# Gate biases as a 3-row product instead of an addition on VectorE, and the turn of the inverses pinned behind a weight split

## The chip, the core and the metric

The kernel runs on one core of a Trainium2 chip. A core has a matrix engine (TensorE, PE in the rows; its weight loads are PEld), a vector engine (VectorE, DVE), a scalar engine for functions (ScalarE, ACT), GpSimd (POOL) and SyncE (SP), which here only issues DMAs. Each engine works through its own instructions in a fixed order and waits at an instruction until its operands are there; all that stands behind it waits too. The metric is the device time of one execution in microseconds (us); the median of three runs is compared.

## What is computed

The reference is a stack of two blocks on 256 tokens of 2048 channels, in fp32. The first has two attention layers. The second is the one that the change touches:

```python
def second_block(x, ...):
    h = rms_norm(x, norm_w[i])
    proj = h @ w_in[i]
    (g_qkv, g_z, g_b, g_a, r_feat, r_z, s_u, s_z, gate_logits) = _split_cols(proj, SPLIT_SIZES)
    o_a = gdn_branch(...)        # gated delta rule in chunks of 64, with triangular solves
    o_b = rwkv7_branch(...)      # a second recurrence with the same kind of solve
    o_c = s5_branch(...)         # a diagonal state space
    branch_proj = einsum('blnc,ncd->blnd', [o_a, o_b, o_c], w_branch[i])
    gates = sigmoid(gate_logits.reshape(bsz, seq, N_BRANCH, D_MODEL) + gate_b[i])
    merged = sum(gates * branch_proj, axis=2)
    x = x + merged @ w_out[i]
    return rms_norm(x, final_norm_w)
```

There are 3 x 2048 gate columns, each with a bias in `gate_b`.

## The kernel before

Nearly all of the work is projections: activations times a weight matrix that is read from HBM. To keep fp32 accuracy, each number is split into a high and a low part, and a projection makes three products (high by high, high by low, low by high) of 512 columns each, or the like of it. The generator `weights` (line 185) loads a projection's weights in parts: a raw part (`raw`, 512 KB, six buffers), a cast to the high part on ACT (`wh`, L167), and a subtraction for the low part on DVE (`wl`, L124), three buffers each. A group of 512 gate columns has 8 such parts of 12 products each. The raw loads go through SP's queue, in a fixed order, among all other loads and stores that SP issues.

`projT` (line 262) is the projection that the gates use: 256 tokens in two halves, accumulated in a PSUM tile `pj` of which there are two, so that one group is evacuated while the next accumulates. `gates` (line 1555) runs it for 12 groups: nine in a row (0, 1, 2, 4, 5, 6, 8, 9, 10), then 11, 7 and 3, each right after a `z_gate` projection and ahead of the branch products that use the result (`in_w_branch`). The activations in SBUF are not yet divided by the norm, so that a group's evacuation multiplies by the token's factor `r` and adds the bias, which a DMA has spread over 128 partitions (`gb`, out of the tile ring `ev` with four buffers), takes tanh of half of it, and stores the result to a DRAM tile `gates`.

Beside the projections, chains of small steps run as generators (`Flow`): the recurrences. Their steps are put into the program by a clock that counts TensorE's columns: `yield LAT["inv"]` means that the chain goes on after 32 us of products. `inverse64` (line 1106) inverts 64 x 64 triangles, six times in the program. It writes them to DRAM and reads their 16 x 16 diagonal blocks (`uim`, `LB`), inverts these in some 20 small DVE operations on `b` (the last is a reduction, L1142), sends the result through DRAM again (`dim`, then two loads of `e`, both on ACT's queue), turns `e` by a transposition on DVE (L1149), and then needs four products with the turned blocks. The first of these, `ps<-e,d`, comes after the `inv` delay.

The order of instructions on each engine is made by a scheduler from priorities; `high_priority(offset=...)` moves weight loads and evacuations ahead, `issue_after(i)` puts what is in its block behind the instruction `i` on the same engine.

Of the kernel before, what the change touches and what calls it, by code (L numbers as in the profile page):

```python
# [8 lines left out]
F32 = mybir.dt.float32  # L9
F32R = mybir.dt.float32r  # L10
AF = mybir.ActivationFunctionType
ALU = mybir.AluOpType
# [10 lines left out]

LAT = dict(small=12.0, bc=8.5, fd=10.0, fb=1.2, fh=0.8, z=0.3, sm=8.85, pt=1.42, st=6.0, ix=0.55, top=9.0, s5=11.0, inv=32.0, pr=1.3,
           prz=1.6, feat=15.0, prod=2.2, c1=1.25, c3=1.3, gn=11.0, sc=6.5, conv=22.5, ln=4.1, rw=2.3, rb=9.0, gp=1.0,
           kt=1.0, gu=3.25, gc=1.3, gR=1.5, go=1.0, gg=7.2)

# [32 lines left out]
class Ker:  # L62
# [122 lines left out]
    def weights(self, w, blocks, nk=KT, pool=None, KC=KC):  # L185
        runs, off = [], 0
        for c0, n in [r for b in blocks for r in (b if isinstance(b, list) else [b])]:
            if runs and runs[-1][0] + runs[-1][1] == c0:
                runs[-1][1] += n
            else:  # L190
                runs.append([c0, n, off])
            off += n
        for kc in range(0, nk, KC):
          self.ahead(kc)
          with self.tc.high_priority(offset=self.HP), self.linked():
            raw = self.t(self.pw, [128, KC, off], "raw", bufs=6)
            for c0, n, o in runs:
                d = self.nc.sync.dma_start(
                    raw[:, :, o:o + n],
                    w[kc * 128:(kc + KC) * 128, c0:c0 + n].rearrange("(k p) c -> p k c", p=128))  # L200
            h, l = (self.t(pool or self.pw, [128, KC, off], tag, F32R, bufs=8 if pool else 3) for tag in ("wh", "wl"))
            i = self.split(h, l, raw)
          if self.order:
              self.order = [d.ins] + i
          yield kc, h, l
# [53 lines left out]
        self.after()  # L259


    def projT(self, w, c0, n, x, evac, nk=KT):
        xh, xl = x
        pt = self.t(self.pp, [128, 2, 512], "pj")
        for kc, h, l in self.weights(w, [(c0, n)], nk):
            for k in range(self.KC):
                kk = kc + k
                for t in range(2):
                    ts = slice(t * 128, t * 128 + 128)
                    st, sp = kk == 0, kk == nk - 1  # L270
                    self.mm(pt[:, t, 0:n], xh[:, kk, ts], h[:, k, 0:n], st, False)
                    self.mm(pt[:, t, 0:n], xh[:, kk, ts], l[:, k, 0:n], False, False)
                    self.mm(pt[:, t, 0:n], xl[:, kk, ts], h[:, k, 0:n], False, sp)
                    self.tick()
        if self.must is not None:
            self.drain(self.must)
        with self.tc.high_priority(offset=self.HPE):
            evac(pt)
        self.after()
# [635 lines left out]
class Block2:  # L915
# [188 lines left out]
    def inverse64(self, pl, usrc, C, turn, n=8):  # L1104
# [41 lines left out]
        for d in range(2):  # L1146
            dma(D2[64 * d:64 * d + 64, 0], at(di, d * n * 4160, [[64, 64], [4160, n], [1, 64]]))
        D2 = [D2[:, 0], D2[:, 1]]
        nc.vector.transpose(D2[1].rearrange("p n s -> p (n s)"), D2[0].rearrange("p n s -> p (n s)"))  # L1149
        d4, c4 = K.t(pl, [128, 2, n, 64], "d4"), K.t(pl, [128, 2, n, 64], "c4")  # L1150
        Uo, NT, Y, Z = d4[:, 0], d4[:, 1], c4[:, 0], c4[:, 1]
        for d in range(2):
            rows = slice(64 * d, 64 * d + 64)
            K.tt(Uo[rows], usrc(d, rows), C["off"][rows].unsqueeze(1).to_broadcast([64, n, 64]), ALU.mult)

        def prod(l, r):
            p = K.ps()
# [3 lines left out]
                    rows = slice(64 * d, 64 * d + 64)  # L1161
                    K.mm(pv[rows, i], l[rows, i], r[rows, i])
            return pv
        yield LAT["inv"]
        nc.scalar.copy(NT, prod(Uo, D2[1]))
        yield LAT["pr"]
        nc.scalar.copy(Y, prod(NT, D2[0]))
# [384 lines left out]
            K.act(self.o[0][:, hs, c * 128:c * 128 + 128], pv4(p), AF.Copy, scale=prm["gnw"])  # L1552


    def gates(self, groups, dst):
        K, nc = self.K, self.nc
        bias = self.a["gate_b_2"][0].rearrange("n c -> (n c)")
        for gi in groups:
            def evac(pt, gi=gi):
                e = K.t(self.pe, [128, 2, 512], "ev")  # L1560
                gb = K.t(self.pe, [128, 2, 512], "ev")[:, 0]
                nc.sync.dma_start(gb, bias[gi * 512:gi * 512 + 512].partition_broadcast(128))
                for t in range(2):
                    K.stt(e[:, t], pt[:, t], self.r[:, t:t + 1], gb, ALU.mult, ALU.add)
                K.act(e, e, AF.Tanh, scale=0.5)
                nc.sync.dma_start(dst[gi], e)
            K.projT(self.w, 10448 + gi * 512, 512, self.x, evac)

    def z_gate(self, pl, i, c0, factor, need=None):
        K = self.K  # L1570
# [99 lines left out]
def second_block(K, x1, yt, w_out1, T, prm):  # L1670
# [39 lines left out]
    with ExitStack() as e2:  # L1710
        gd = K.t(K.pd, [12, 128, 2, 512], "gates")
        with ExitStack() as e3:
            B = Block2(K, xt, r2, rbc, e3)
            pcn = K.pool("b2c", 1, e3)
            C = block2_consts(K, pcn, prm)
            pr = K.pool("rec", 1, e3)
            B.images(pr)
            e4 = ExitStack()
            ps5 = K.pool("s5", 1, e4)
            f, wl, al, baz, rn, feats = B.rwkv_feats(pcn, prm, C)  # L1720
            B.out(1)
            gq = K.t(K.pd, [24, 128, S], "gqkv")
            feats(0)
            nf, nr = [1], [0]

            def chains():
                for q in range(4):
                    while nf[0] <= q:
                        yield 1.0
                    yield from B.rwkv(pr, q, f, wl, al, rn, prm, C)  # L1730
                    nr[0] += 1
                B.out(0)
                sc = yield from B.gdn_scalars(pcn, baz, C)
                while B.nq < 6:
                    yield 1.0
                for hf in range(2):
                    yield from B.gdn(pr, hf, gq, sc, prm, C)
                    yield
            main = K.flow(chains(), (0,))
            B.s5_u()  # L1740
            side = K.flow(B.s5(ps5, T, prm), (1,))
            for q in range(1, 4):
                feats(q)
                nf[0] = q + 1
            for g in range(6):
                B.gdn_qkv(gq, (g,))
            B.gates((0, 1, 2, 4, 5, 6, 8, 9, 10), gd)
            K.drain(side)
            B.s5_glu(prm)
            for i, n in enumerate(("d_o0", "d_o1", "d_o2")):  # L1750
                if n in a:
                    nc.sync.dma_start(a[n].rearrange("b p s -> p b s"), B.o[i])
            e4.close()
            pz = K.pool("zs", 1, e3)
            acc = K.t(K.pd, [4, 128, 2, 512], "acc")
            o2 = B.z_gate(pz, 2, 9424, 0.125)
            B.gates((11,), gd)
            B.branch(2, o2, gd, acc)
            while nr[0] < 4:
                main.step()  # L1760
            o2 = B.z_gate(pz, 1, 7376, 0.5)
            B.gates((7,), gd)
            B.branch(1, o2, gd, acc)
            o2 = B.z_gate(pz, 0, 3072, 0.5, lambda g: K.drain(main, g + 1))
            K.drain(main)
            B.gates((3,), gd)
            m = K.xtiles("x")
            B.branch(0, o2, gd, acc, m)
# [120 lines left out]
```

## Time and profile before

| | |
|---|---|
| median of three runs | 2176.87 us (2176.57 to 2179.06) |
| profiled execution | 2182.66 us |
| its span, first to last instruction | 2180.6 us |
| busy share of PE, DVE, ACT, POOL | 97%, 77%, 48%, 2% |
| granted clock of TensorE, mean | 0.992 |
| DMA | 440 MB at 202 GB/s |

The durations below come from the one profiled execution. A row of a timeline says when an instruction began, how long it took, its engine (a small q is the engine's queue, which issues a DMA), its line in the kernel, what it writes and reads (buffer numbers left out), and, in brackets, how long the engine had idled before and what ended that.

### The profile page before, as it was taken

How to read it: one execution, taken by the hardware profiler on the slowest of the kernel's cores; microseconds unless marked ns; L12 is line 12 of the kernel's file. 1: busy time of each engine (PE TensorE's matmuls, PEld its weight loads, DVE VectorE, ACT ScalarE, POOL GpSimd, SP SyncE). 2: the span in 40 equal slices, each digit the busy share in tenths (PEclk: the TensorE clock that was granted, in tenths of full speed). 3: DMA queues.
4: the chain of work that ended last, by engine and by line, in shares of the span. 5: the costliest groups of instructions: out<-in, count | busy, mean ns of one | idle time of the engine just before them, and what ended most of it. 6: DMA issues, size and time to landing. Idle time of an engine off the chain costs nothing. (4 is left out here: it accounts for less than half of the span.)

```text
span 2180.6 us, 32801 instructions
## 1 busy us (share of the span) xinstructions
PE 2120.5 (97%) x12275; PEld 1792.8 (82%) x12275; DVE 1670.1 (77%) x2919; ACT 1043.7 (48%) x1498; POOL 53.5 (2%) x113
## 2 busy tenths in 40 slices
PE   9999999999999999999999999999999989989998
PEld 8888898888898888888888778777678868868886
DVE  6788866668999777565789999989888848765665
ACT  5445554544454455555544434334346635525443
POOL 2001000000000000000000000000000000000000
PEclk9999999999999999999999999999999999999999
DMA  7666656766667756876676676665856657775874
GB/s 251 196 181 176 170 155 184 245 207 213 203 180 206 221 158 183 279 221 197 191 223 199 196 207 206 202 206 177 230 164 191 195 190 208 237 215 156 274 231 148
DMA packets 356143, 440.09 MB, mean 202 GB/s; under 512 B 50380, under 2 KB 262528, under 8 KB 355664
## 3 DMA queue, kind: packets, MB, share of 16 engines
q1 hardware_dynamic: 328240, 430.81, 65.4%
q10 hardware_dynamic: 26512, 4.68, 1.2%
q0 software_dynamic: 1232, 2.51, 0.4%
q8 instruction: 96, 1.57, 0.3%
q14 instruction: 63, 0.52, 0.1%
HBM read 396.35 MB, written 41.57 MB: 201 GB/s over the span
## 5 line engine op out<-in xcount | busy, mean ns | idle before, releaser
L167 ACT CAST wh<-raw 128x1024 fp32r<-128x1024 f32 (+4 forms) x668 | 683.8, 1026 | 857.1 <-PE pj L141 713.6
L124 DVE TENSOR_TENSOR wl<-raw,wh 128x1024 fp32r<-128x1024 f32 (+4 forms) x668 | 794.3, 1191 | 341.1 <-ACT wh L167 332.8
L141 PE MATMUL pj<-x,wh 128*128 128x512 f32 (+3 forms) x3008 | 1019.2, 387 | 0.7 <-ACT wh L167 0.7
L141 PE MATMUL pj<-x,wl 128*128 128x256 f32 (+2 forms) x2864 | 807.4, 282 | 2.3 <-DVE wl L124 2.3
L141 PEld LDWEIGHTS pj<-x,wh 128*128 128x128 f32 (+2 forms) x3008 | 554.2, 187 | 125.7 <-issue 9.2
L141 PEld LDWEIGHTS pj<-x,wl 128*128 128x128 f32 (+2 forms) x2864 | 539.9, 189 | 9.0 <-issue 4.0
L141 PE MATMUL pj<-wh,x 128*128 128x512 f32 (+2 forms) x1472 | 451.2, 382 | 0.0
L141 PEld LDWEIGHTS pj<-wh,x 128*128 128x128 f32 x1472 | 271.8, 189 | 46.6 <-issue 2.9
L141 PE MATMUL pj<-wl,x 128*128 128x512 f32 (+2 forms) x736 | 279.5, 380 | 1.2 <-DVE wl L124 1.2
L141 PEld LDWEIGHTS pj<-wl,x 128*128 128x128 f32 x736 | 138.6, 188 | 25.7 <-DVE wl L124 2.1
L141 PE MATMUL pj<-wh,y 128*128 128x512 f32 x512 | 158.4, 390 | 0.0
L141 PEld LDWEIGHTS pj<-wh,y 128*128 128x128 f32 x512 | 95.9, 188 | 19.8
L141 PE MATMUL pj<-wl,y 128*128 128x512 f32 x256 | 99.9, 390 | 0.0
L141 PE MATMUL pj<-wl,E 128*128 128x512 f32 x192 | 77.2, 402 | 2.6 <-DVE wl L124 2.6
L141 PE MATMUL pj<-wh,E 128*128 128x512 f32 x192 | 77.4, 403 | 2.1 <-ACT wh L167 2.1
L141 PE MATMUL pj<-wh,G 128*128 128x512 f32 x192 | 77.1, 402 | 0.0
L124 DVE TENSOR_TENSOR raw<-y 128x256 f32<-128x256 f32 (+7 forms) x256 | 64.0, 289 | 3.0
L141 PEld LDWEIGHTS pj<-wl,y 128*128 128x128 f32 x256 | 48.1, 188 | 9.9
L124 DVE TENSOR_TENSOR y<-raw 128x128 f32<-128x128 f32 (+7 forms) x256 | 46.2, 223 | 2.5
L141 PEld LDWEIGHTS pj<-wl,E 128*128 128x128 f32 x192 | 36.7, 191 | 12.0 <-DVE wl L124 4.8
L141 PEld LDWEIGHTS pj<-wh,E 128*128 128x128 f32 x192 | 36.6, 191 | 10.4 <-ACT wh L167 2.5
L124 DVE TENSOR_TENSOR s5w<-ps,s5tb 128x512 f32<-128x512 f32 x64 | 42.6, 683 | 3.2 <-PE ps L141 3.1
(457 smaller groups left out, 1998.3 us busy)
## 6 DMA issues: line engine op xcount, KB each, us to landing
raw<-in_w_in_dram SPq DMA_DIRECT2D x460, 512.0 KB, 3.7
raw<-in_w_out_dram SPq DMA_DIRECT2D x96, 512.0 KB, 4.7
raw<-in_w_branch_dram SPq DMA_DIRECT2D x48, 512.0 KB, 4.6
raw<-in_w_in_dram SPq DMA_DIRECT2D x24, 344.0 KB, 3.2
s5t<-y SPq DMA_DIRECT2D x16, 512.0 KB, 5.7
s5tb<-s5t SPq DMA_DIRECT2D x32, 256.0 KB, 3.6
raw<-in_w_in_dram SPq DMA_DIRECT2D x16, 384.0 KB, 3.6
gates<-ev SPq DMA_DIRECT2D x12, 512.0 KB, 3.6
```

The source lines that it names most:

```text
L124: return (eng or self.nc.vector).tensor_tensor(out=out, in0=a, in1=b, op=op)
L141: i = self.nc.tensor.matmul(out, l, r, start=st, stop=sp, **k)
L167: i = self.nc.scalar.copy(h, src)
```

## The change

It has two parts. The gate biases enter as the first product of a group's accumulation: three rows (high, high and low part of the bias against the high, low and high part of the tokens' divisors 1/r), so that ACT can make the tanh straight from PSUM with a factor r/2 per token. A new function `gate_bias` prepares both once: the biases' parts are written to a DRAM tile `gbr`, and each group loads its three rows of 512 (6 KB) from there into an `ev` tile. In the inverses, the transposition is moved behind the `inv` delay, which grows from 32 to 34 us, and is pinned behind the latest weight split on DVE (`lastw`); a further delay `turn` of 2.5 us lies between it and the first product.

```diff
@@ -23,7 +23,7 @@
 
 
 
-LAT = dict(small=12.0, bc=8.5, fd=10.0, fb=1.2, fh=0.8, z=0.3, sm=8.85, pt=1.42, st=6.0, ix=0.55, top=9.0, s5=11.0, inv=32.0, pr=1.3,
+LAT = dict(small=12.0, turn=2.5, bc=8.5, fd=10.0, fb=1.2, fh=0.8, z=0.3, sm=8.85, pt=1.42, st=6.0, ix=0.55, top=9.0, s5=11.0, inv=34.0, pr=1.3,
            prz=1.6, feat=15.0, prod=2.2, c1=1.25, c3=1.3, gn=11.0, sc=6.5, conv=22.5, ln=4.1, rw=2.3, rb=9.0, gp=1.0,
            kt=1.0, gu=3.25, gc=1.3, gR=1.5, go=1.0, gg=7.2)
 
@@ -200,6 +200,7 @@
                     w[kc * 128:(kc + KC) * 128, c0:c0 + n].rearrange("(k p) c -> p k c", p=128))
             h, l = (self.t(pool or self.pw, [128, KC, off], tag, F32R, bufs=8 if pool else 3) for tag in ("wh", "wl"))
             i = self.split(h, l, raw)
+            self.lastw = i[1]
           if self.order:
               self.order = [d.ins] + i
           yield kc, h, l
@@ -259,15 +260,18 @@
         self.after()
 
 
-    def projT(self, w, c0, n, x, evac, nk=KT):
+    def projT(self, w, c0, n, x, evac, nk=KT, bias=None):
         xh, xl = x
         pt = self.t(self.pp, [128, 2, 512], "pj")
+        if bias is not None:
+            for t in range(2):
+                self.mm(pt[:, t, 0:n], bias[0][t], bias[1], True, False)
         for kc, h, l in self.weights(w, [(c0, n)], nk):
             for k in range(self.KC):
                 kk = kc + k
                 for t in range(2):
                     ts = slice(t * 128, t * 128 + 128)
-                    st, sp = kk == 0, kk == nk - 1
+                    st, sp = kk == 0 and bias is None, kk == nk - 1
                     self.mm(pt[:, t, 0:n], xh[:, kk, ts], h[:, k, 0:n], st, False)
                     self.mm(pt[:, t, 0:n], xh[:, kk, ts], l[:, k, 0:n], False, False)
                     self.mm(pt[:, t, 0:n], xl[:, kk, ts], h[:, k, 0:n], False, sp)
@@ -1146,12 +1150,15 @@
         for d in range(2):
             dma(D2[64 * d:64 * d + 64, 0], at(di, d * n * 4160, [[64, 64], [4160, n], [1, 64]]))
         D2 = [D2[:, 0], D2[:, 1]]
-        nc.vector.transpose(D2[1].rearrange("p n s -> p (n s)"), D2[0].rearrange("p n s -> p (n s)"))
         d4, c4 = K.t(pl, [128, 2, n, 64], "d4"), K.t(pl, [128, 2, n, 64], "c4")
         Uo, NT, Y, Z = d4[:, 0], d4[:, 1], c4[:, 0], c4[:, 1]
         for d in range(2):
             rows = slice(64 * d, 64 * d + 64)
             K.tt(Uo[rows], usrc(d, rows), C["off"][rows].unsqueeze(1).to_broadcast([64, n, 64]), ALU.mult)
+        yield LAT["inv"]
+
+        with K.tc.issue_after(K.lastw):
+            nc.vector.transpose(D2[1].rearrange("p n s -> p (n s)"), D2[0].rearrange("p n s -> p (n s)"))
 
         def prod(l, r):
             p = K.ps()
@@ -1161,7 +1168,7 @@
                     rows = slice(64 * d, 64 * d + 64)
                     K.mm(pv[rows, i], l[rows, i], r[rows, i])
             return pv
-        yield LAT["inv"]
+        yield LAT["turn"]
         nc.scalar.copy(NT, prod(Uo, D2[1]))
         yield LAT["pr"]
         nc.scalar.copy(Y, prod(NT, D2[0]))
@@ -1552,19 +1559,44 @@
             K.act(self.o[0][:, hs, c * 128:c * 128 + 128], pv4(p), AF.Copy, scale=prm["gnw"])
 
 
+    def gate_bias(self):
+
+
+        K, nc = self.K, self.nc
+        self.gbr = K.t(K.pd, [12, 3, 512], "gbr")
+        b = K.t(self.pe, [128, 2, 512], "ev")[0:12, 0]
+        nc.sync.dma_start(b, self.a["gate_b_2"][0].rearrange("n (q c) -> (n q) c", c=512))
+        bp = K.t(self.pe, [128, 2, 512], "ev", F32R)[0:12]
+        K.split(bp[:, 0], bp[:, 1], b)
+        for i, part in enumerate((0, 0, 1)):
+            nc.sync.dma_start(self.gbr[:, i], bp[:, part].bitcast(F32))
+        inv, h, c = K.t(K.pc, [128, 2], "rinv"), K.t(K.pc, [128, 2, 2], "rinvp", F32R), K.t(K.pc, [128, 2, 3], "rinvc")
+        nc.vector.reciprocal(inv, self.r)
+        K.split(h[:, 0], h[:, 1], inv)
+        for i, part in enumerate((0, 1, 0)):
+            nc.vector.tensor_copy(c[:, :, i], h[:, part].bitcast(F32))
+        p = K.ps()
+        self.rdiv = []
+        for t in range(2):
+            K.tr(p[0:3, 128 * t:128 * t + 128], c[:, t])
+            self.rdiv.append(K.t(K.pc, [128, 128], "dg", F32R, bufs=2)[0:3])
+            nc.scalar.copy(self.rdiv[t], p[0:3, 128 * t:128 * t + 128])
+        self.rhalf = K.t(K.pc, [128, 2], "rhalf")
+        K.ts(self.rhalf, self.r, 0.5, None, ALU.mult)
+
     def gates(self, groups, dst):
         K, nc = self.K, self.nc
-        bias = self.a["gate_b_2"][0].rearrange("n c -> (n c)")
         for gi in groups:
+            with K.tc.high_priority(offset=K.HP):
+                gb = K.t(self.pe, [128, 2, 512], "ev")[0:3, 0]
+                nc.sync.dma_start(gb, self.gbr[gi])
+
             def evac(pt, gi=gi):
                 e = K.t(self.pe, [128, 2, 512], "ev")
-                gb = K.t(self.pe, [128, 2, 512], "ev")[:, 0]
-                nc.sync.dma_start(gb, bias[gi * 512:gi * 512 + 512].partition_broadcast(128))
                 for t in range(2):
-                    K.stt(e[:, t], pt[:, t], self.r[:, t:t + 1], gb, ALU.mult, ALU.add)
-                K.act(e, e, AF.Tanh, scale=0.5)
+                    K.act(e[:, t], pt[:, t], AF.Tanh, scale=self.rhalf[:, t:t + 1])
                 nc.sync.dma_start(dst[gi], e)
-            K.projT(self.w, 10448 + gi * 512, 512, self.x, evac)
+            K.projT(self.w, 10448 + gi * 512, 512, self.x, evac, bias=(self.rdiv, gb.bitcast(F32R)))
 
     def z_gate(self, pl, i, c0, factor, need=None):
         K = self.K
@@ -1721,6 +1753,7 @@
             B.out(1)
             gq = K.t(K.pd, [24, 128, S], "gqkv")
             feats(0)
+            B.gate_bias()
             nf, nr = [1], [0]
 
             def chains():
```

What moved is seen in three places of the program. The first is SP's queue at the gate group 11. `raw` of `in_w_in` are the group's weight loads, `raw` of `in_w_branch` those of the branch products that follow, `ev<-in_gate_b` and `ev<-gbr` the load of the group's bias. Before:

```order
L198 DMA raw_16676<-in_w_in_dram 128x2x512
L198 DMA raw_16730<-in_w_in_dram 128x2x512
L198 DMA raw_16766<-in_w_in_dram 128x2x512
L198 DMA raw_16803<-in_w_in_dram 128x2x512
L198 DMA raw_16849<-in_w_branch_dram 128x2x512
L1562 DMA ev_16842<-in_gate_b_dram 128x512
L198 DMA raw_16885<-in_w_branch_dram 128x2x512
L198 DMA raw_16909<-in_w_branch_dram 128x2x512
```

After:

```order
L198 DMA raw_16751<-in_w_in_dram 128x2x512
L198 DMA raw_16769<-in_w_in_dram 128x2x512
L198 DMA raw_16792<-in_w_branch_dram 128x2x512
L1592 DMA ev_16638<-gbr_10051 3x512
L198 DMA raw_16810<-in_w_branch_dram 128x2x512
L1415 DMA b_2918_17380<-gqkv_9854 128x4x256
L198 DMA raw_16829<-in_w_branch_dram 128x2x512
```

The bias load, smaller now and from another place, stands behind the first weight load of the next projection in both. Such is its place in groups 11, 7 and 3; in the eight others after the first, it comes behind the group's eighth weight load, and in the first one behind its fourth.

The second place is TensorE at the beginning of the same group: `pj` is the accumulator, `x` the activations, `wh` and `wl` the split weights; `ev` is the loaded bias and `dg` the turned divisors. Before:

```order
L141 MATMUL pj_16505<-x_8492,wl_16575 128x256
L141 MATMUL pj_16505<-x_8492,wh_16574 128x512
L141 MATMUL pj_16505<-x_8492,wl_16575 128x256
L141 MATMUL pj_16603<-wh_16606,x_8492 128x512
L141 MATMUL pj_16603<-wl_16607,x_8492 128x512
L141 MATMUL pj_16603<-wh_16606,x_8492 128x512 x2
L141 MATMUL pj_16603<-wl_16607,x_8492 128x512
```

After:

```order
L141 MATMUL pj_16501<-x_8492,wh_16609 128x512
L141 MATMUL pj_16501<-x_8492,wl_16610 128x256
L141 MATMUL pj_16640<-ev_16638,dg_10071 128x512
L141 MATMUL pj_16640<-ev_16638,dg_10074 128x512
L141 MATMUL pj_16640<-wh_16645,x_8492 128x512
L141 MATMUL pj_16640<-wl_16646,x_8492 128x512
L141 MATMUL pj_16640<-wh_16645,x_8492 128x512 x2
```

Two products that read the loaded bias are now ahead of the group's first product with weights.

The third place is DVE in the fifth inverse, from the last reduction on `b` to the transposition of `e`. `wl` are weight splits of the projections beside it, and the row at L127 with `r` is a gate group's evacuation. Before:

```order
L1142 TENSOR_REDUCE b_2741_16364<-b_2741_16364 64x8x8
L124 TENSOR_TENSOR wl_16852<-raw_16849,wh_16851 128x1024
L124 TENSOR_TENSOR wl_16888<-raw_16885,wh_16887 128x1024
L127 SCALAR_TENSOR_TENSOR ev_16841<-pj_16603,r_1500_9225,ev_16842 128x512 x2
L124 TENSOR_TENSOR wl_16912<-raw_16909,wh_16911 128x1024
L124 TENSOR_TENSOR wl_16951<-raw_16948,wh_16950 128x1024
L1149 STREAM_TRANSPOSE e_2743_16390<-e_2743_16390 128x512
L124 TENSOR_TENSOR wl_16974<-raw_16971,wh_16973 128x1024
L124 TENSOR_TENSOR c_2745_16395<-ps_2796_16745,e_2743_16390 128x512
```

After:

```order
L1146 TENSOR_REDUCE b_2770_16518<-b_2770_16518 64x8x8
L124 TENSOR_TENSOR wl_16700<-raw_16697,wh_16699 128x1024
L124 TENSOR_TENSOR wl_16718<-raw_16715,wh_16717 128x1024
L124 TENSOR_TENSOR wl_16736<-raw_16733,wh_16735 128x1024
L124 TENSOR_TENSOR wl_16754<-raw_16751,wh_16753 128x1024
L124 TENSOR_TENSOR wl_16772<-raw_16769,wh_16771 128x1024
L124 TENSOR_TENSOR wl_16795<-raw_16792,wh_16794 128x1024
L124 TENSOR_TENSOR wl_16813<-raw_16810,wh_16812 128x1024
L1161 STREAM_TRANSPOSE e_2772_16544<-e_2772_16544 128x512
L124 TENSOR_TENSOR wl_16832<-raw_16829,wh_16831 128x1024
```

The transposition has gone from behind four weight splits to behind seven, and the evacuation's rows are gone.

## Rows read from the trace of the kernel before

**Rows 1.** The page: the span, and part 1, busy time of the engines.

```profile
span 2180.6 us, 32801 instructions
...
PE 2120.5 (97%) x12275; PEld 1792.8 (82%) x12275; DVE 1670.1 (77%) x2919; ACT 1043.7 (48%) x1498; POOL 53.5 (2%) x113
```

**Rows 2.** Chain of waits, TensorE's own: us in total, times, longest.

```profile
PE ps L141 <- DVE e L1149: 20.6, 5, 6.9
PE pj L141 <- DVE wl L124: 6.2, 9, 1.1
```

**Rows 3.** The line of the transposition: what its engine idled for (us, times).

```profile
  DMA e<-dim: 21.7, 6
```

**Rows 4.** Timeline around the fifth inverse, all engines.

```profile
1745.22 0.68 DVE L1142 TENSOR_REDUCE b<-b 64x64 f32<-64x512 f32 x1
...
1760.41 0.71 DVE L1149 STREAM_TRANSPOSE e<-e 128x512 f32<-128x512 f32 x1 [6.92 <-DMA e<-dim]
...
1761.17 1.12 PE L141 MATMUL ps<-e,d 64*64 64x64 f32 x16 [6.86 <-DVE e L1149]
```

**Rows 5.** Stretches after TensorE's waits: length, PE busy, PEclk, DMA share, GB/s.

```profile
1430.60:1436.00 5.40, 5.40 (x54) 0.57 0.80 271
...
1938.00:1944.50 6.50, 6.47 (x59) 0.55 0.66 174
1278.60:1283.00 4.40, 4.35 (x84) 1.00 0.78 231
```

**Rows 6.** Chain of waits of ACT, and of SP's queue.

```profile
ACT wh L167 <- PE pj L141: 713.6, 450, 7.0
...
SPq L198 <- DVE wl L124: 1046.4, 457, 9.8
```

**Rows 7.** Timeline of PE and SP, begin of groups 11 and 3.

```profile
1726.46 0.39 PE L141 MATMUL pj<-wh,x 128*128 128x512 f32 x1
1726.69 0.40 PE L141 MATMUL pj<-wl,x 128*128 128x512 f32 x1
...
1729.30 0.46 SPq L1562 DMA_DIRECT2D ev<-in_gate_b_dram  x1
...
2014.88 0.40 PE L141 MATMUL pj<-wh,x 128*128 128x512 f32 x1
...
2017.72 0.46 SPq L1562 DMA_DIRECT2D ev<-in_gate_b_dram  x1
```

**Rows 8.** Timeline of SP and DVE, begins of two of the other groups.

```profile
1393.50 0.47 SPq L1562 DMA_DIRECT2D ev<-in_gate_b_dram  x1
...
1397.39 0.74 DVE L127 SCALAR_TENSOR_TENSOR ev<-pj,r,ev 128x512 f32<-128x512 f32 x1
...
1618.93 0.46 SPq L1562 DMA_DIRECT2D ev<-in_gate_b_dram  x1
...
1619.71 1.41 DVE L127 SCALAR_TENSOR_TENSOR ev<-pj,r,ev 128x512 f32<-128x512 f32 x2 [0.29 <-PE pj L141]
```

**Rows 9.** DMA issues: KB each, median us from issue to landing.

```profile
raw<-in_w_in_dram SPq DMA_DIRECT2D x460, 512.0 KB, 3.7
...
ev<-in_gate_b_dram SPq DMA_DIRECT2D x12, 256.0 KB, 4.2
...
y<-in_norm_dram SPq DMA_DIRECT2D x1, 8.0 KB, 1.6
```

**Rows 10.** Stretch of group 3: length, busy of PE, PEld, DVE, ACT, POOL.

```profile
2014.00:2037.00 23.00, 23.00 (x104) 19.08 (x104) 15.62 (x15) 11.08 (x12) 0.00 (x0) 1.00 0.64 199
```

**Rows 11.** Groups by line: busy, mean ns of one, idle before, releaser.

```profile
L167 ACT CAST wh<-raw 128x1024 fp32r<-128x1024 f32 (+4 forms) x668 | 683.8, 1026 | 857.1 <-PE pj L141 713.6
L124 DVE TENSOR_TENSOR wl<-raw,wh 128x1024 fp32r<-128x1024 f32 (+4 forms) x668 | 794.3, 1191 | 341.1 <-ACT wh L167 332.8
...
L136 ACT ACTIVATE ev<-ev 128x1024 f32<-128x1024 f32 x18 | 19.0, 1058 | 6.4 <-DVE ev L124 3.8 <-DVE ev L127 2.6
...
L127 DVE SCALAR_TENSOR_TENSOR ev<-pj,r,ev 128x512 f32<-128x512 f32 x24 | 17.1, 743 | 1.8 <-PE pj L141 1.6
```

## The prediction

> **What bounds the kernel now.** I began with the busy rows: TensorE is busy in 97% of the span [rows 1], so the bound is the row of matrix products, and a change is worth what it adds to that row or takes out of its gaps. Of about 60 us of gaps, the list of TensorE's waits names one large cause: 20.6 us in five waits for the turn of the inverses (DVE's transposition of `e`), while all waits of the projections (`pj`) for weight splits come to 6.2 us [rows 2]. The transposition waited 21.7 us for its DMAs [rows 3]: DVE stands at it, and TensorE's next instruction stands behind DVE. In the fifth inverse the last reduction begins at 1745.22 (ends 1745.9), the turn at 1760.41 after 6.92 us of idling, and TensorE has stood for 6.86 us [rows 4]. From the end of the reduction to the turn that is 14.5 us.
>
> A stall costs more than its length. After the waits in the third to sixth inverse (3.3 to 6.9 us) the granted clock fell to its lower level of 1.2 GHz for a while: a mean of 0.57 over 5.4 us in the first of these four, of 0.55 over 6.5 us in the last; after the wait in the second inverse (1.6 us) it stayed at 1.00 [rows 5]. Stretch times one minus the clock gives 5.4 x 0.43 = 2.3 and 6.5 x 0.45 = 2.9 us, and 9.5 us for all four, 2.4 each. So the inverses cost 20.6 + 9.5 = 30.1 us.
>
> The last view is of what paces the loads. ACT's casts wait for TensorE (713.6 us), and the queue that issues the weights waits for DVE's splits (1046.4 us) [rows 6]. Thus TensorE's own progress sets when a load is issued: six raw buffers and three split buffers are a ring.
>
> **The change, part by part.**
>
> *Bias products.* Each of the 12 gate groups gets two more products of 512 columns. Such a product starts 0.23 us after the one before (1726.46 to 1726.69 [rows 7]): 24 x 0.23 = 5.5 us. No product of 3 rows stands in the trace; bounds are 0 and this 128-row spacing, and I take the spacing, since the width is the same. The Trainium skill ("TensorE: Matmul & The Clock Gate", Why this matters for your kernels) says that a single product with 32 rows takes as long as one with 128; by that it is 5.5 us too, and no run here shows it.
>
> *The bias load: the deciding term.* Before, the bias was needed at a group's end, some 20 us after its load. Now it is the first operand of the group, since its product opens the accumulation. But the order of SP's queue hardly moves: in 8 groups the new load stands behind the group's eighth and last weight load, in three (11, 7, 3) behind the next projection's first as well; only in the first group is it earlier (behind the fourth). Those weight loads can't be issued early. The eighth needs the second's raw buffer, hence the second split, hence a split buffer that TensorE frees only with the previous group's seventh part; the ninth needs the eighth part of the previous group to be finished.
>
> The old load stood at the same places, so its rows tell when. In the three late groups TensorE began the first at 1726.46 and the last at 2014.88, and their loads were issued at 1729.30 and 2017.72: 2.84 us later in both [rows 7]. In the eight others I compare its issue with the previous group's evacuation, which starts when that group ends: 1393.50 against 1397.39 in the first, 1618.93 against 1619.71 in the last; the mean of the eight is -1.0 us [rows 8], about -0.8 against TensorE's own start. To this comes the time to landing. It was 4.2 us for the old load of 256 KB, 3.7 for a weight load of 512 KB, and 1.6 for the smallest one (8 KB, in a quiet place) [rows 9]. The new load has 6 KB, but stands right behind a 512 KB load; I take that one's 3.7, and 1.6 and 4.2 as ends. So TensorE waits 8 x (3.7 - 0.8) = 23 us and 3 x (2.84 + 3.7) = 20 us: 43 us together, from 8 x 0.8 + 3 x 4.4 = 20 up to 8 x 3.4 + 3 x 7.0 = 48. What is behind the wait on TensorE is the whole group. In the stretch of a late group, 2014 to 2037, TensorE was busy for 23.00 of 23.00 us [rows 10], so there is nothing for it to eat into.
>
> The Trainium skill ("DMA: Bandwidth & Descriptors", Anatomy of one DMA) gives a DMA about 2.0 us plus its bytes over 436 GB/s, which would land 6 KB in 2.0 us; the rows behind a weight load show 4.2 us for 256 KB, where that rule makes 2.6, so here it is too short. By it the waits would be 8 x 1.2 + 3 x 4.8 = 24 us.
>
> *Clock.* The three long waits exceed those that brought the low level above: 3 x 2.4 = 7 us. The eight of 2.9 us lie between the 1.6 us that cost nothing and the 3.3 us that did: 0 to 19 us, I take 8. Together 15, ends 7 and 26.
>
> *The turn.* In DVE's order the weight splits between the last reduction and the turn were 4, 4, 3, 3, 4 and 3 in the six inverses and are now 7, 6, 2, 6, 7 and 3. A split belongs to 12 products, 12 x 0.23 = 2.8 us of TensorE, so 6 or 7 cover 17 to 19 us, more than the 14.5 needed; DVE no longer stands there in inverses 2, 4 and 5. In the third it gets shorter, in the sixth not longer (though the product itself comes 2.5 us later by the table). In the third, bias waits push TensorE back too. I leave 8.5 us of the 30.1 (6 of wait, 2.5 of clock) and book -21.6; ends -15 and -30.
>
> *DVE and ACT.* 24 fused multiply-adds of 743 ns leave DVE, 17.8 us; ACT's one tanh of 1024 columns per group (1058 ns [rows 11]) becomes two of 512, little more in sum. Both lie beside the products, since each group accumulates in the other of two buffers. TensorE's waits for splits (6.2 us [rows 2]) can shrink: -2, ends 0 and -6. If that cover went, the whole 17.8 us would count as gain, but DVE isn't what the groups end on.
>
> *Setup.* `gate_bias` runs once beside projections: two small transpositions and a few DVE operations, 1 us, ends 0 and 3.
>
> Sum: 5.5 + 43 + 15 - 21.6 - 2 + 1 = **+41 us**. Against the profiled execution (2182.66 us, span 2180.6 [rows 1]) that is 2224; it lay 5.8 above the median of the runs, 2176.87, so for a median I say **2218 us**.
>
> **The rivals.**
>
> *Small loads land soon.* If 6 KB overtakes the weights and lands in 2.0 us, waits are 24 us, clock 7 (long ones only): 5.5 + 24 + 7 - 21.6 - 2 + 1 = +14, 2191 us. For it speaks the 1.6 us row; against it, that the old load, in the same places, took 4.2.
>
> *The turn does not deliver.* DVE's order is pinned behind a split that TensorE paces; if the turn still ends last and all 30.1 us stay, the sum is 5.5 + 43 + 15 + 1 - 2 = +63, 2239 us. For it: inverse 3 lost a split of distance. Against: 6 or 7 splits elsewhere.
>
> *Faster: the loads come ahead of need.* DVE, freed of 17.8 us, makes the second split earlier, so the eighth load goes out before the group's start by more than its landing time, and the eight waits vanish. It decides from an issue 1.6 us ahead at the shortest landing, 3.7 ahead at mine. Left are 3 x 4.4 = 13 of waits and 7 of clock: 5.5 + 13 + 7 + 1 - 30 - 6 = -9, 2168 us. Against it: the split can't start before TensorE's seventh part ends, 2.8 us before the group, and cast and split take 1.0 and 1.2 us [rows 11] after that.
>
> **How the numbers follow.** Forecast (2204 to 2232) 0.52; small loads land soon 0.24; the turn does not deliver 0.14; loads ahead 0.10. Range 2188 to 2240: it takes in the first two with their bounds and most of the third, and leaves the faster case out. About 0.2%, 4 us, is what can be told from no change. Of the last rival 0.07 ends faster and 0.03 within 0.2%, with 0.02 more from the low end of the second: faster 0.07, same 0.05, slower 0.88.
>
> **What would show it.** In the new profile TensorE's waits should name the small load (`ev<-gbr`) in about 11 waits, three of 5 to 7 us and eight of 1 to 4, 43 us in all, and the granted clock should dip behind the long ones, around the three groups ahead of the branch products above all. The waits for the turn should fall from 20.6 to about 6 us, and the transposition should no longer wait for its DMAs in inverses 2, 4 and 5. The bias rows should show a spacing of 0.23 us. The prediction is wrong if the small loads land before their groups start, or if the weight loads ahead of them go out much sooner than in the trace of before.

## The result

The changed kernel took 2215.05 us, median of 5 runs (2211.7 to 2221.18), against 2178.29 us before (5 runs, 2176.57 to 2179.6): a ratio of 1.0172, 95% interval 1.0156 to 1.0189, that is 36.8 us slower. The prediction was 2218.

The page of the changed kernel, span and busy rows, which answer to [rows 1]:

```profile
span 2215.6 us, 32825 instructions
...
PE 2143.0 (97%) x12301; PEld 1808.2 (82%) x12301; DVE 1656.7 (75%) x2902; ACT 1046.3 (47%) x1514; POOL 51.2 (2%) x113
```

The span grew by 35.0 us. Of this, 22.5 are longer busy time of TensorE and 12.5 more idle time (2215.6 - 2143.0 = 72.6 against 60.1). Busy time grows by the 24 added products and when the clock is low. The clocks of the cores, of the changed kernel:

```profile
core 0: 2215.6 us, clock 0.983
```

Over the whole span 2215.6 x 0.017 = 38 us of clock were lost, against 2180.6 x 0.008 = 17 before: 20 us more. TensorE's waits in the changed kernel (us in total, times, longest), which answer to [rows 2]:

```profile
PE pj L141 <- DMA ev<-gbr: 15.5, 4, 5.9
PE ps L141 <- DVE s5w L124: 6.7, 5, 2.8
PE ps L141 <- DVE s5x L124: 6.2, 3, 5.0
PE ps L147 <- DVE up L124: 5.8, 1, 5.8
...
PE ps L147 <- ACT LB L136: 2.7, 1, 2.7
PE ps L147 <- DVE RW L127: 2.6, 1, 2.6
...
PE ps L141 <- DVE e L1161: 0.7, 1, 0.7
```

The wait for the turn is all but gone (20.6 to 0.7), and the new wait for the bias row is there, but under its own name it has only 15.5 us in four waits where I had forecast 43 in about 11. Next to it stand waits that the kernel before had less of or not at all: s5x, up, LB, RW. So the total alone doesn't tell whether the prediction was right for its own reasons. The first place to look is the start of group 11 and of group 3, in the timeline of SP and of PE:

```profile
1755.01 0.37 SPq L198 DMA_DIRECT2D raw<-in_w_branch_dram  x1
1755.43 0.34 SPq L1592 DMA_DIRECT2D ev<-gbr  x1
...
1752.48 0.28 PE L141 MATMUL pj<-x,wl 128*128 128x256 f32 x1
1758.62 1.19 PE L141 MATMUL pj<-ev,dg 3*128 3x512 f32 x2 [5.86 <-DMA ev<-gbr]
...
2042.09 0.37 SPq L198 DMA_DIRECT2D raw<-in_w_branch_dram  x1
2042.51 0.34 SPq L1592 DMA_DIRECT2D ev<-gbr  x1
...
2039.54 0.28 PE L141 MATMUL pj<-x,wl 128*128 128x256 f32 x1
2045.65 1.09 PE L147 MATMUL ps<-ident,up 128*128 128x128 f32 x4 [5.83 <-DVE up L124]
2046.67 1.22 PE L141 MATMUL pj<-ev,dg 3*128 3x512 f32 x2
```

In both, TensorE ran dry 2.7 us before the row was issued (1752.76 and 1755.43; 2039.82 and 2042.51), close to the 2.84 of [rows 7], right behind the ninth weight load. In group 11 the wait carries the row's name. In group 3 the order has four turns of `up` ahead of the bias products; they started 1.0 us before these, and the wait carries the name of `up`, though the row's issue and the hole are the same. Whether that hole belongs to the row is a question for an experiment.

### The profile page after: what moved, and what is told of

Same layout as the page of the kernel before. It is cut to its first block, busy times and chain, and to the rows that moved or that the text cites. A ratio compares the mean times of both kernels' runs of the same rounds, so it can differ in the third digit from the quotient of the medians.

```text
span 2215.6 us, 32825 instructions
## 1 busy us (share of the span) xinstructions
PE 2143.0 (97%) x12301; PEld 1808.2 (82%) x12301; DVE 1656.7 (75%) x2902; ACT 1046.3 (47%) x1514; POOL 51.2 (2%) x113
## 5 line engine op out<-in xcount | busy, mean ns | idle before, releaser
L141 PE MATMUL pj<-wh,x 128*128 128x512 f32 (+2 forms) x1472 | 467.1, 392 | 0.1
L141 PEld LDWEIGHTS pj<-wh,x 128*128 128x128 f32 x1472 | 282.4, 195 | 56.5 <-issue 8.1
L141 PE MATMUL pj<-wl,x 128*128 128x512 f32 (+2 forms) x736 | 285.9, 388 | 1.3 <-DVE wl L124 1.3
L141 PEld LDWEIGHTS pj<-wl,x 128*128 128x128 f32 x736 | 143.3, 195 | 24.8 <-DVE wl L124 2.1
```

Source lines behind the costliest of these rows:

```text
L141: i = self.nc.tensor.matmul(out, l, r, start=st, stop=sp, **k)
```

## The experiments

Theory A: the loss is the bias row's lateness at the groups' starts, with the clock behind it, whatever name the holes carry; the turn's change is a gain by itself. Theory B: the row costs what its name shows, and the new waits for s5x, up, LB and RW come from the turn's new place. Each ratio is against the kernel before in the same set of runs. It took 2181.29 us (8 runs) beside the first four experiments; 2180.95 (17) beside the one without the bias, the delay alone, the pin alone and the delay of 38; 2179.85 (7) beside the three rows ahead, the delay of 27 and both repairs.

**The turn alone.** The kernel before with the second half of the change (34 and 2.5):

```diff
-        nc.vector.transpose(D2[1]..., D2[0]...)
...
+        yield LAT["inv"]
+        with K.tc.issue_after(K.lastw):
+            nc.vector.transpose(D2[1]..., D2[0]...)
...
+        yield LAT["turn"]
```

> The kernel before with the change of the inverses alone (the transposition pinned behind the last weight split, its delays 34 and 2.5). In the changed kernel TensorE's waits for the turn were 0.7 us instead of 20.6, and the clock's low stretches behind them (13.6 us of lost clock before) were gone. Theory A (the bias row costs everything that was lost, the turn delivers on its own): about 30 us faster than before, 2140 to 2155, waits for the turn below 3 us. Theory B (DVE's chains, which the turn used to hold back, are late next: the new waits of the changed kernel for s5x, up, LB and RW, some 17 us, with low clock behind them, belong to the turn's new place): within 10 us of before, 2170 to 2185.

Measured: 2161.25 us, ratio 0.9907 (0.9888 to 0.9927), 20.0 us faster. That lies between the two ranges, 6 us above A's and 9 below B's. What speaks against theory B is the waits: LB and RW have none of note, s5x is below 0.5 us and up has 1.4. The gain is less than the 26 to 41 us that theory A gave; 6.8 us of waits for the turn were left, which the whole change didn't show:

```profile
PE ps L141 <- DVE e L1158: 6.8, 3, 4.9
```

**The bias alone.** The changed kernel with the inverses of before (delay 32):

```diff
-LAT = dict(... inv=34.0, ...)
+LAT = dict(... inv=32.0, ...)
...
+        nc.vector.transpose(D2[1]..., D2[0]...)
...
-        yield LAT["inv"]
-        with K.tc.issue_after(K.lastw):
-            nc.vector.transpose(D2[1]..., D2[0]...)
...
-        yield LAT["turn"]
+        yield LAT["inv"]
```

> The changed kernel with the inverses as they were before (delay 32, no pin): the bias change alone. Theory A: it carries the whole loss and the turn's stall too: 60 to 75 us slower than before, 2235 to 2255, with waits for the turn of about 20 us back. Theory B: only the named waits for the small load (15.5 us), 5.5 us of products and some clock: 20 to 35 us slower than before, 2197 to 2212, and no new waits for s5x, up, LB and RW.

Measured: 2231.11 us, ratio 1.0227 (1.021 to 1.0244), 49.8 us slower. That lies between the two ranges, nearer to A. Its waits:

```profile
PE pj L141 <- DMA ev<-gbr: 19.9, 6, 6.0
PE ps L141 <- DVE e L1153: 13.7, 3, 6.2
...
PE ps L141 <- DVE G L124: 5.7, 1, 5.7
```

The turn is waited for 13.7 us and not 20.6. Why is open: the waits went in the third inverse (5.2 to 0.1) and in the sixth (3.3 to 0), and in neither was a row issued or waited for between the last reduction and the turn. The 5.7 us for G lie right ahead of the bias product of group 7 (1915.30), whose row was issued at 1910.22 (the hole ends at 1913.30): again a hole of the late groups' length under another name, and here with the old inverses, so that such holes don't come from the turn's new place.

**The rows loaded ahead.** The changed kernel with each row loaded one group, or one z projection, ahead, in the same ring:

```diff
+    def gate_row(self, gi):
+        with K.tc.high_priority(offset=K.HP):
+            self.gb = K.t(self.pe, [128, 2, 512], "ev")[0:3, 0]
+            K.nc.sync.dma_start(self.gb, self.gbr[gi])
...
-        for gi in groups:
-            with K.tc.high_priority(offset=K.HP):
-                gb = K.t(self.pe, [128, 2, 512], "ev")[0:3, 0]
-                nc.sync.dma_start(gb, self.gbr[gi])
+        for j, gi in enumerate(groups):
+            gb = self.gb
+            if j + 1 < len(groups):
+                self.gate_row(groups[j + 1])
...
+            B.gate_row(11)
             o2 = B.z_gate(pz, 2, 9424, 0.125)
```

> The changed kernel with each group's bias row loaded one group (or one z projection) ahead, in the same ring of buffers; products and turn unchanged. Theory A (the loss is the row's lateness at a group's start, and the clock behind those waits): waits for the row go from 15.5 us to under 2, lost clock falls by some 15 to 20 us, the whole is faster than the kernel before: 2145 to 2165. Theory B: only the named 15.5 us and a part of the clock come back: 2190 to 2200.

Measured: 2165.82 us, ratio 0.9936 (0.9914 to 0.9958): faster than before, 0.8 us above A's range, and 49.4 us shorter in span than the changed kernel. Page, clock and TensorE's longest wait:

```profile
span 2166.2 us, 32839 instructions
...
PE 2122.6 (98%) x12301; PEld 1792.6 (83%) x12301; DVE 1653.5 (76%) x2902; ACT 1046.0 (48%) x1514; POOL 49.7 (2%) x113
...
core 0: 2166.2 us, clock 0.996
...
PE ps L141 <- DVE e L1161: 7.3, 4, 4.8
```

Idle time falls from 72.6 to 43.6 us and busy time by 20.4: 29.0 + 20.4 = 49.4. The wait for `ev<-gbr` is out of the list, and with it go those of 5.0 us for s5x, 5.8 for up, 2.7 for LB and 2.6 for RW. Waits for the turn come back in part (7.3 us against 0.7). So the holes without the row's name go when the row is early. One of them side by side, the stretch at the third group's start (length, PE, PEld, DVE, ACT, POOL busy, PEclk, DMA share, GB/s), first of the changed kernel, then with the rows ahead:

```profile
1425.00:1433.00 8.00, 2.99 (x12) 1.53 (x10) 7.23 (x11) 2.45 (x4) 0.00 (x0) 0.78 0.61 178
```

```profile
1425.00:1433.00 8.00, 8.00 (x35) 6.17 (x34) 8.00 (x14) 4.04 (x5) 0.00 (x0) 1.00 0.66 207
```

TensorE was busy for 2.99 of 8 us against 8.00, the clock at 0.78 against 1.00. TensorE's order in this place, first of the changed kernel, then with the rows ahead:

```profile
1431.89 1.06 PE L141 MATMUL ps<-s5x,ct 128*32 128x256 f32 x2 [5.01 <-DVE s5x L124]
1432.88 0.79 PE L141 MATMUL pj<-ev,dg 3*128 3x512 f32 x1
```

```profile
1425.25 0.73 PE L141 MATMUL pj<-ev,dg 3*128 3x512 f32 x2
...
1435.30 0.62 PE L141 MATMUL ps<-s5x,ct 128*32 128x256 f32 x2 [0.69 <-DVE s5x L124]
```

So the wait's name was not false: in the changed kernel the products with `s5x` stand ahead of the bias product, and DVE ended the first `s5x` only at 1431.83. With the rows ahead `s5x` is ready even later (1435.25) and costs 0.69 us, since 10 us of the group's products are put ahead of it. The edit has made the row early and has changed the order with it; no run here parts the two. The same holds for `up` in group 3, which DVE ended at 2045.51 and which does not read the row.

**The bias last.** The changed kernel with the bias products at the end of each accumulation, the rows where the change had them:

```diff
-        if bias is not None:
-            for t in range(2):
-                self.mm(pt[:, t, 0:n], bias[0][t], bias[1], True, False)
...
+                    if kk == nk - 1 and bias is not None:
+                        self.mm(pt[:, t, 0:n], bias[0][t], bias[1], False, True)
```

> The changed kernel with the bias products as the last of each accumulation and not the first; the row is loaded where it was, so it has a group's 20 us to land. Theory A: as with rows loaded early, 2145 to 2165, and no wait for the row at a group's start. Theory B: 2190 to 2200. If this one and the one with rows loaded ahead differ by more than 5 us, the place of the products matters for something else than the row's landing.

Measured: 2172.73 us, ratio 0.9955 (0.9938 to 0.9972): faster than before, but 6.9 slower than rows ahead, and outside the range. It bears A out by another way: the same products and the same loads, only needed 20 us later. For the 6.9 us the rows have two causes. One is the waits for the turn, 9.2 us against 7.3. The other is the products: at the end of a group the two bias products stand apart, each between products of 128 rows. The timeline of PE, first with the rows ahead (group 3), then with the bias last (group 7):

```profile
1976.62 0.28 PE L141 MATMUL pj<-x,wl 128*128 128x256 f32 x1
1976.74 0.39 PE L141 MATMUL pj<-x,wh 128*128 128x512 f32 x1
1976.97 0.28 PE L141 MATMUL pj<-x,wl 128*128 128x256 f32 x1
1977.18 0.73 PE L141 MATMUL pj<-ev,dg 3*128 3x512 f32 x2
1977.84 0.50 PE L141 MATMUL pj<-wh,x 128*128 128x512 f32 x1
1978.17 0.39 PE L141 MATMUL pj<-wl,x 128*128 128x512 f32 x1
```

```profile
1881.31 0.40 PE L141 MATMUL pj<-wh,x 128*128 128x512 f32 x1
1881.64 0.49 PE L141 MATMUL pj<-ev,dg 3*128 3x512 f32 x1
1882.06 0.50 PE L141 MATMUL pj<-wh,x 128*128 128x512 f32 x1
1882.40 0.40 PE L141 MATMUL pj<-wl,x 128*128 128x512 f32 x1
```

A pair takes 0.66 us from its start to the next product, that one 0.33 instead of 0.23, and the product ahead of the pair 0.21 (1976.97 to 1977.18) where its like took 0.12 (1976.62 to 1976.74): 0.09 + 0.66 + 0.10 = 0.85. A single one makes the spacing ahead of it 0.33, its own 0.42 and the one behind 0.34 where 0.23 is usual: 0.10 + 0.42 + 0.11 = 0.63 each, against 0.85 / 2 = 0.42 in a pair. With the rows ahead nine of the twelve groups have such a pair (in three the order has other products between the two), which makes 18 x 0.21 = 3.8 of the 6.9 us, an estimate from these spacings.

**Three rows ahead.** Only the rows of groups 11, 7 and 3 loaded ahead:

```diff
         for gi in groups:
+            if len(groups) > 1:
+                self.gate_row(gi)
+            gb = self.gb
...
+            B.gate_row(11)
             o2 = B.z_gate(pz, 2, 9424, 0.125)
```

> The changed kernel with only the rows of the three late groups (11, 7, 3) loaded ahead, before the projection in front of them; the nine others stand where the change put them. In the changed kernel TensorE idled 5.2, 4.7 and 5.2 us around these three rows and lost 3.4, 5.1 and 3.4 us of clock there; loading all rows ahead gave 49 us. If each group pays for itself: 15 us of idle and 8 to 12 of clock come back, 2187 to 2196. If the three long waits carry nearly all the loss: 2165 to 2180. If the time comes back as waits elsewhere: above 2200.

Measured: 2200.46 us, ratio 1.0093 (1.0076 to 1.0109): 14.6 us faster than the changed kernel by the medians (17 by the ratios). That is 4 us over the first range and, by 0.5 us, in the third case, where the time comes back as waits elsewhere. The three holes are gone, but a part was given back, and the hole for s5x at the third group, whose row is still late, has stayed:

```profile
PE pj L141 <- DMA ev<-gbr: 9.7, 3, 6.1
PE ps L141 <- DVE e L1161: 6.3, 3, 4.2
PE ps L141 <- DVE s5x L124: 6.2, 3, 5.2
```

With group 11's hole gone, the order has only three splits between reduction and turn in the fifth inverse, and TensorE waited 4.2 us there; in the changed kernel there were seven and no wait.

**Without the bias.** To price the products and DVE's relief, the changed kernel without the rows' loads and without the bias products; the gates lack their biases:

```diff
-            with K.tc.high_priority(offset=K.HP):
-                gb = K.t(self.pe, [128, 2, 512], "ev")[0:3, 0]
-                nc.sync.dma_start(gb, self.gbr[gi])
...
-            K.projT(..., evac, bias=(self.rdiv, gb.bitcast(F32R)))
+            K.projT(..., evac)
```

> The changed kernel without the bias row's loads and without the 24 bias products, so its gates lack their biases (a part of the computation is left out); the tanh from the accumulator by ACT and the 24 multiply-adds less on DVE stay. With rows loaded early the kernel took 2165.8, the turn change alone 2161.3. If the products cost their 5.5 us and DVE's relief is worth next to nothing: 2157 to 2163, within 3 us of the turn change alone. If DVE's 17.8 us were worth something by themselves: below 2155. If the products were free and the setup or the loads cost the 4.5 us: 2164 to 2168.

Measured: 2162.26 us, ratio 0.9899 (0.9876 to 0.9923). That is the turn alone (2161.25) within its noise, although DVE has 24 multiply-adds less than there: its 17.8 us are worth nothing to be seen here. Against rows ahead (2165.82) the products cost 3.6 us by the medians; by their spacings it is 12 x 0.85 = 10 us. The profiled run without bias lost more clock (mean 0.994 against 0.996, 4 us), which would cover a part; the rest is not reconciled.

**Delay or pin.** The turn's change has two halves. First the delay alone, an edit of the kernel before:

```diff
-LAT = dict(... inv=32.0, ...)
+LAT = dict(... inv=36.5, ...)
```

> The kernel before with the inverses' delay of 32 raised to 36.5 (the sum of the two new ones) and nothing pinned: DVE still reaches the transposition early and stands there for its DMAs. Theory A (what counts is how much of TensorE's work lies between the last reduction and the first product): as fast as the turn change alone, 2156 to 2167. Theory B (the pin counts, since a standing DVE makes splits late): TensorE's waits move to the weight splits, 2168 to 2182.

Then the pin with the products' old delay, an edit of the turn alone:

```diff
-LAT = dict(... inv=34.0, ...)
+LAT = dict(... inv=29.5, ...)
```

> The turn change alone with its first delay cut from 34 to 29.5, so that the products come by the same table as before (29.5 + 2.5 = 32) and only the pin is new. Theory A (delay counts): waits for the turn of 15 to 20 us remain, 2174 to 2184. Theory B (pin counts): 2158 to 2168.

Measured: the delay alone 2174.2 us, ratio 0.9962 (0.9947 to 0.9978), some 7 us faster; the pin alone 2151.89, ratio 0.9852 (0.9828 to 0.9875), 29 us faster and 6 below B's range. Theory A here, that the delay counts, falls by both. B's sign for the delay alone did not show, though: the waits did not move to the splits, 13.8 us of them stayed with the turn. The pin alone is the fastest kernel of this study. The fifth inverse with the delay alone, on DVE and PE:

```profile
1750.53 1.22 DVE L124 TENSOR_TENSOR wl<-raw,wh 128x1024 fp32r<-128x1024 f32 x1 [0.67 <-ACT wh L167]
1758.93 0.71 DVE L1149 STREAM_TRANSPOSE e<-e 128x512 f32<-128x512 f32 x1 [7.17 <-DMA e<-dim]
1759.56 1.18 DVE L124 TENSOR_TENSOR wl<-raw,wh 128x1024 fp32r<-128x1024 f32 x1
...
1752.36 0.39 PE L141 MATMUL pj<-wh,G 128*128 128x512 f32 x1
1759.69 1.11 PE L141 MATMUL ps<-e,d 64*64 64x64 f32 x15 [6.94 <-DVE e L1149]
```

DVE stands at the transposition for 7.17 us, and the next split is behind it. TensorE used up the last split (done at 1751.75) and then had nothing left to do: 6.94 us, as in [rows 4]. More delay puts little work between reduction and product when that work's own operands wait behind the turn. With the pin alone:

```profile
1729.65 1.22 DVE L124 TENSOR_TENSOR wl<-raw,wh 128x1024 fp32r<-128x1024 f32 x1
1730.79 0.70 DVE L1158 STREAM_TRANSPOSE e<-e 128x512 f32<-128x512 f32 x1
...
1731.54 1.15 PE L141 MATMUL ps<-e,d 64*64 64x64 f32 x32 [0.36 <-DVE e L1158]
```

DVE makes five splits, turns without a stand, and TensorE waits 0.36 us.

**More delay, less delay.** The turn alone with its first delay at 38 and at 27 (29.5 was above, 34 is the change):

```diff
-LAT = dict(... inv=34.0, ...)
+LAT = dict(... inv=38.0, ...)
```

> The turn change alone with the first delay raised from 34 to 38. In the turn change alone the fifth inverse still had 4 splits between reduction and turn, TensorE waited 4.9 us there and 1.6 in the sixth, with 3.4 us of clock lost behind the first. Theory A: these go, 2150 to 2158. Rival: the chain ends later and the work that needs the inverses is late, or it meets another chain on DVE: 2161 to 2175.

```diff
-LAT = dict(... inv=34.0, ...)
+LAT = dict(... inv=27.0, ...)
```

> The pin alone with the first delay cut further, from 29.5 to 27. If distance is what delivers and 29.5 (4 to 6 splits, no wait) is near the edge: one split less in some inverses, 3 to 10 us of waits for the turn back, 2155 to 2165. If an earlier end of the chain is what made 29.5 better than 34: 2143 to 2152.

Measured: 2160.43 us, ratio 0.9896 (0.9873 to 0.9918), and 2168.95, ratio 0.9945 (0.9924 to 0.9967). With 38 the waits for the turn fell to 2.0 us, but the time did not: it lies between the two ranges, within 1 us of the delay of 34, and waits for splits and casts were 9.4 us (8.6 with 34 and 4.8 with 29.5). So theory A falls; of the rival's causes none was singled out. With 27, 5.1 us of waits for the turn came back, as forecast, but the time is 4 us above the range. What the six inverses did, counted from the timelines (34 and 27 were timed in other sets, beside 2181.29 and 2179.85 before):

| kernel | splits between last reduction and turn, six inverses | TensorE's waits for the turn | us |
|---|---|---|---|
| before | 4, 4, 3, 3, 4, 3 | 20.6 | 2180.95 |
| delay 36.5, no pin | 4, 4, 3, 4, 4, 4 | 13.8 | 2174.2 |
| pin, 27 | 5, 4, 5, 4, 5, 4 | 5.1 | 2168.95 |
| pin, 29.5 | 6, 6, 5, 5, 5, 4 | 0.4 | 2151.89 |
| pin, 34 | 7, 6, 3, 5, 4, 4 | 6.8 | 2161.25 |
| pin, 38 | 12, 5, 4, 5, 6, 4 | 2.0 | 2160.43 |

The pin stands behind whatever split is the latest when the chain's step comes up, so the number of splits depends on where in a projection that is, not on the delay alone: with 34 the third and fifth inverse got 3 and 4.

**Both repairs.** All rows ahead and the first delay at 29.5:

```diff
-LAT = dict(... inv=34.0, ...)
+LAT = dict(... inv=29.5, ...)
```

> All rows loaded ahead, and the pin with the shorter delay (29.5 in place of 34). If the two parts add up: 2165.8 less the 9.4 us between the turn change alone and the pin alone, 2153 to 2160, still some 4 us slower than the pin alone, for the products. If the shorter delay's gain was a matter of where splits happen to fall: 2160 to 2170.

Measured: 2168.76 us, ratio 0.9951 (0.9931 to 0.9971). The parts don't add up; the second case held. The third to fifth inverse have 3 splits each and waits of 1.2, 1.2 and 3.4 us. So 29.5 isn't a better delay as such; by the counts of splits it suits the order that the program without the bias products happens to have.

## Why the prediction was right, and where it wasn't

The chain of runs gives each part its price: the turn alone -20.0 us, the bias with the rows on time +4.6 (2165.82 against 2161.25), the rows' lateness the rest of the +36.8, 52 us (49.4 between the two spans).

That 2218 came so near to 2215.05 is in part luck. The bias with all that hangs on it was booked at 5.5 + 43 + 15 - 2 + 1 = 62.5 us and is worth 49.8 alone; the turn was booked at -21.6 and brings -13.0 on top of the bias (36.8 - 49.8). One error of 13 us and one of 9 the other way leave 4.

*The bias load* was the deciding term, and it decided. I had booked 43 of waits and 15 of clock, 58 together; loading ahead gave back 49.4, as 29.0 of idle time and 20.4 of busy time, which is mostly the low clock, since the products are the same. In the late groups the place was right (issued 2.6 to 2.7 us after TensorE ran dry, 2.84 forecast), but in group 11 the first product came 3.2 us after the issue, not 3.7; TensorE's gaps beside the three rows were 5.9, 5.3 and 5.8 us, 17 in place of 20. In the eight others they sum to 20 us in place of 23, but unevenly, from none to 5.8. Of these 37 us loading ahead gave back 29.0 net, as 6.6 us of waits for the turn came back beside it. What the new profile was to show came true only in part: the row's name has 15.5 us, not 43, because the order has steps of the chains ahead of the bias products, and TensorE stands for these. That a late row changes the order, too, is not in the prediction.

*Clock.* I gave the eight middle waits 8 us and the three long ones 7, together 15; the busy time that came back was 20.4. Behind the hole of 5.0 us at the third group the mean was 0.51 over 8.1 us, behind the three late rows 0.57, 0.53 and 0.60, each from the end of the hole on. Stretch times one minus the clock gives 4.0, 2.8, 4.3 and 2.5 us; I had taken 2.4 from [rows 5]. In rows (length, PE busy, PEclk, DMA share, GB/s):

```profile
1431.90:1440.00 8.10, 8.10 (x19) 0.51 0.81 252
1758.60:1765.00 6.40, 6.38 (x16) 0.57 0.01 3
1898.90:1908.00 9.10, 9.10 (x23) 0.53 0.29 117
2045.70:2052.00 6.30, 6.30 (x18) 0.60 0.00 0
```

*The turn.* -21.6 booked, -20.0 measured alone, with 6.8 us of waits left where I had left 6. The reason was right, splits between the reduction and the turn; what I hadn't seen is that the pin alone brings all of it and more (29 us), while more delay alone brings 7. In the whole change the turn's gain is smaller, 13 us: with the bias alone only 13.7 us of waits for the turn are left to be saved, in place of 20.6.

*The bias products* cost more than booked by their spacings: 0.85 us a pair, 10 in place of 5.5; by the medians it is 3.6, as said above. I had taken the 128-row spacing of 0.23. The Trainium skill ("TensorE: Matmul & The Clock Gate", Why this matters for your kernels) says that a single product with 32 rows takes as long as one with 128. No run here times a product by itself; among 128-row products one with 3 rows took longer to the next start (0.42 us against 0.23). Another page of the Trainium skill ("TensorEngine Tiling (Array Packing)", Key Properties) says that a change of the tiling mode drains TensorE, without a price. Whether a 3-row product changes the mode no run here shows; the longer spacing at each step between 3 and 128 rows would fit, but the pair's inner step, from 3 rows to 3, is long too (0.34), so it would not explain all.

*DVE's relief and the setup* were booked at -2 and +1; the run without bias shows both together within 1 us.

*The rivals.* Small loads landing soon (2191) failed: in the four waits that carry the row's name its first product came 3.2 to 4.2 us after the issue. The fit that the prediction names for it from the Trainium skill ("DMA: Bandwidth & Descriptors", Anatomy of one DMA) stands there for DMAs that GpSimd issues, and these go by SP's queue. The turn that doesn't deliver was refuted by the waits of 0.7. The rows ahead of need did not happen by themselves, but that rival's mechanism is what the experiment built, and its kernel took 2165.82; I had worked out 2168 for it, with 13 us of waits and 7 of clock left and more from the turn than there was, so that nearness is luck.

## What to carry to other kernels

An operand that moves from the end of an accumulation to its start needs its load moved as well: here a load of 6 KB in its old place cost 50 us, and asking for it a group earlier gave them back. On an engine that works in order, an instruction that waits for a DMA holds up all that feeds the bottleneck behind it (DVE stood for 7.17 us, TensorE for 6.94); here moving it behind a few pieces of that feed was worth 29 us, giving the DMA more time by the table 7. And a stall's name is only the last thing waited for: to see what a late operand costs, make it early and compare idle time, clock and the order, since other steps may have been put into its hole, and taking one away may uncover another.

The best version found is the kernel before with the pin alone and delays of 29.5 and 2.5: 2151.89 us, 1.5% faster than before. How firmly that number holds for other delays is open, since it depends on where the splits fall (2152 to 2169 us over four delays).

## What the runs showed of the hardware that was unexpected

A 3-row product of 512 columns between 128-row products takes 0.42 us to the next start when alone and 0.33 in a pair, where 0.23 is usual for the same 512 columns. The 128-row products right ahead of it and behind it are spaced longer, too, by about 0.1 us each.
